# Low parts of the first two weight tiles of five stages: subtracted on GpSimd instead of added by a transfer

## The chip, the cores and the metric

One core of a Trainium2 chip runs the whole program. A core has a matrix engine (TensorE, PE in the rows; PEld is its loading of weights), three engines for elementwise work (VectorE or DVE, ScalarE or ACT, GpSimd or POOL), an engine that here only issues transfers (SyncE, SP), and DMA queues that move data. Each engine works its instructions off in order and waits on semaphores for what it needs from others. The metric is the time on the device in microseconds; the number compared is the median of several runs.

## The reference

Two layers of a transformer-like trunk. Each layer is a feed-forward block, a mixer and another feed-forward block, all of them added onto x:

```python
def ffn_sublayer(x, mod, k, g, w_in, w_out):
    h = modulated_norm(x, mod, k, g)
    gt, up = jnp.split(h @ w_in, 2, axis=-1)
    return x + 0.5 * mod[:, None, 3 * k + 2] * ((jax.nn.silu(gt) * up) @ w_out)

def trunk_layer(...):
    x = ffn_sublayer(x, mod, 0, norm_g[0], w_ffn_in[0], w_ffn_out[0])
    h = modulated_norm(x, mod, 1, norm_g[1])
    q, k, v, u_pool, u_conv, bg, cg = jnp.split(h @ w_in, IN_SPLITS, axis=-1)
    ...
    y = jnp.concatenate([attn, pool, conv], axis=-1) @ w_out
    x = x + mod[:, None, 5] * y
    x = ffn_sublayer(x, mod, 2, norm_g[2], w_ffn_in[1], w_ffn_out[1])
```

D_MODEL is 1024, D_FF 2816. The 128 context rows and the 512 latent rows share the weights, so the kernel treats them as 640 columns. Everything is float32.

## The kernel before

**Products in three parts.** A float32 weight tile is split into a high part wh, which TensorE's fast float32 form holds exactly, and a low part wl, the rest. An activation h is split the same way. `mm3` issues three matmuls for each product: wh times h's high part (L352), wh times h's low part (L353), wl times h's high part (L354). The 640 columns are worked in two halves of 320 (hf 0 and 1); x, transposed, lies in eight tiles of 128 x 640, x0 to x7.

**Where a weight's parts come from.** `load_cols` loads a tile of 128 x 1024 values into a buffer raw (an issue on SP, L181), and `split_w` splits it. ACT writes wh as a rounding copy of raw (L170). Without an engine given, ACT then writes wl = -wh (L173) and POOL issues a transfer that adds raw onto wl in memory (L174, the software queue q0). With an engine given, that engine computes wl = raw - wh in one instruction (L176). There are four buffers each for wh and wl and five for raw; a raw buffer is free for the next load when the adding transfer (or the subtraction) has read it.

**The stages.** ffn(0,0) to 530 us, mixer 0 to 755, ffn(0,2) to 1224, ffn(1,0) to 1681, mixer 1 to 1907, ffn(1,2) to the end. Each of the last five begins while the one before it ends: `update_x` adds the last products onto x tile by tile (DVE, L518, reading PSUM), `add_square` squares the tile on ACT (L251) and sums the squares on DVE (L252), TensorE sums over partitions (L375), and `rsqrt_newton` (ACT L361, DVE L362 to L364) makes the factor of the norm. A stage's first four weight tiles are loaded and split in the same microseconds.

**The head of a mixer.** Its h is made by DVE (L401, tmp from x), ACT (L416, high part) and DVE (L417, low part). The first `project` works two tiles of columns from 1024 on and two from 1536 on, four weight tiles in all.

**The head of an ffn.** h is made for two x tiles at a time (`seven`): DVE L480 and ACT L483 write full, ACT L473 copies the high part of the pair and DVE L474 subtracts the low part. The first pairs of the first half are made before the stage before has quite ended. `ups_by_half(0, 2)` takes the four weight tiles (j, s) with j and s 0 and 1, through `weights(j, s)`. The first ffn has another head (`first_tiles`).

**What sets the order.** The program is written in stages, but a scheduler with prices of its own sets the order of instructions on each engine's queue. Buffers come from pools, and an instruction waits on semaphores for its operands and buffers.

Of the kernel before, what the change touches and what calls it, by code (L numbers as in the profile page):

```python
# [17 lines left out]
P = 128  # L18
# [7 lines left out]
DFF = 2816  # L26
# [70 lines left out]
def trunk_kernel(ctx: ExitStack, tc: tile.TileContext, i: dict, o: dict):  # L97
    nc = tc.nc
# [18 lines left out]
    def slot(dt=F32, name="slot", shape=(2, T)):  # L117
        return slots.tile([P, *shape], dt, tag="slot", name=name)
# [17 lines left out]
    for b in range(T // P):  # L136
        s = slot(name="xin", shape=(D,))
# [26 lines left out]
    def split_w(raw, nk, width, eng=None):  # L164

        view = lambda t: t[:, : nk * width].rearrange("p (k c) -> p k c", k=nk)
        size, tag = (1024, "") if nk * width > 512 else (512, "s")
        h = view(whp.tile([P, size], F32R, tag="wh" + tag, name="wh", bufs=4 if tag == "" else 2))
        lo = view(wlp.tile([P, size], F32R, tag="wl" + tag, name="wl", bufs=4 if tag == "" else 2))
        nc.scalar.activation(h, raw, AF.Copy)  # L170
        if eng is None:

            nc.scalar.activation(lo, f32(h), AF.Copy, scale=-1.0)  # L173
            nc.gpsimd.dma_start(lo, raw, accum_op=ALU.add)  # L174
        else:
            eng.tensor_tensor(lo, raw, f32(h), op=ALU.subtract)  # L176
        return h, lo

    def load_raw(src, c0, width=P, raw=None):
        return raw_w(  # L180
            lambda raw: nc.sync.dma_start(raw, src[:, c0 : c0 + width].rearrange("(k p) c -> p k c", p=P)),  # L181
            src.shape[0] // P,
            width,
            raw,
        )
# [4 lines left out]
    def load_cols(src, c0, width=P, eng=None):  # L190
        return split_w(*load_raw(src, c0, width), eng)
# [364 lines left out]
    def ffn(l, f, n, hs, side, finish, nxt, first=None):  # L556
        w_in = i["w_ffn_in"][l, f]
# [1 line left out]
        gs = {}  # L559

        def weights(j, s):
            return load_cols(w_in, s * DFF + j * P)

        def part(ps, w, hf):

# [25 lines left out]
        def ups_by_half(j0, j1):  # L591

            ws = {(j, s): weights(j, s) for j in range(j0, j1) for s in range(2)}
            for hf in range(2):
                for j in range(j0, j1):
                    ps = [acc(), acc()]
                    for s in range(2):
                        for _ in part(ps[s], ws[j, s], hf):
                            pass
                    gated(j, hf, *ps)  # L600

        def up(j):
            ps = {}
            for s in range(2):
                w = weights(j, s)
                runs = []
                for hf in range(2):
                    ps[s, hf] = acc()
                    runs.append(part(ps[s, hf], w, hf))
                for _ in zip(*runs):  # L610
                    pass
            bias = None
            if first:
                bias, _ = shift_products(ps[0, 1], ps[1, 1])
            for hf in range(2):
                gated(j, hf, ps[0, hf], ps[1, hf], bias)
# [140 lines left out]
    def mixer(l, hs, finish, nxt):  # L757
# [19 lines left out]
        w_in = i["w_in"][l]  # L777
# [17 lines left out]
        def project(*tiles):  # L795

            runs = [(t, (hf,)) for hf in range(2) for t in tiles] if len(tiles) > 1 else [(tiles[0], (0, 1))]
            for ((wh, wl), evac), halves in runs:
                ps = {hf: acc() for hf in halves}
                for k in range(KD):  # L800
                    for hf in halves:
                        mm3(ps[hf][:, :HALF], wh[:, k, :], wl[:, k, :], *hs.part(k, hf), k == 0, k == KD - 1)
                    tick()
                for hf in halves:
                    evac(hf, ps[hf])

        def copy_to(dst):
            def evac(hf, ps):
                a, b = HALVES[hf]
                nc.scalar.activation(dst[:, a:b], ps[:, :HALF], AF.Copy)  # L810

            return evac


        u = slot(name="u")
# [5 lines left out]
        def product_to(m):  # L821
            def evac_z(hf, ps):
                a = HALVES[hf][0]
                for s, e, j in SEGS[hf]:
                    d = s + 2 - j
                    nc.vector.tensor_tensor(
                        zs[m][:, d : d + e - s], ps[:, s - a : e - a], u[:, m, s:e], op=ALU.mult
                    )

            return evac_z  # L830

        project(
            *[(load_cols(w_in, 1024 + m * P), copy_to(u[:, m, :])) for m in range(2)],
            *[(load_cols(w_in, 1536 + m * P), product_to(m)) for m in range(2)],
        )
        for m in range(2):
# [499 lines left out]
    for x, (l, n) in enumerate(steps):  # L1336
        last = x == len(steps) - 1
        fast = not last and steps[x + 1][1] != 1
        new = Seven() if fast else Plain()
        if last:  # L1340
            nxt = output
        else:
            heads = []

            def nxt(hf, t):
                if t < KD - 1:
                    return
                heads.append(norm_head(hf))
                if hf == 1 and fast:
                    seven(*steps[x + 1], new, heads)  # L1350
                elif hf == 1:
                    for h in range(2):
                        norm_tail(*steps[x + 1], h, new, heads[h])

        finish = nothing if last else squares
        if n == 1:
            mixer(l, hs, finish, nxt)
        else:
            ffn(l, n // 2, n, hs, spread(budget.get((l, n), 0), 1 if x else 4, x == 0), finish, nxt, None if x else first_tiles)
        hs = new  # L1360
# [30 lines left out]
```

## Time and profile before

| what | before |
|---|---|
| median of 3 runs | 2360.88 us (2357.27 to 2363.95) |
| the profiled execution | 2359.89 us |
| its span | 2358.1 us |
| granted TensorE clock, mean of the span | 0.993 |
| TensorE busy | 2302.1 us (98%) |
| VectorE busy | 1526.2 us (65%) |
| ScalarE busy | 1055.0 us (45%) |
| GpSimd busy | 123.9 us (5%) |
| adding transfers wl<-raw | 102 of 512 KB |

The profiled execution lies 1.0 us below the median. The page's "idle before" of a group of instructions says how long its engine stood just before them and for whom; of an engine that is busy 98% of the span, each such microsecond is one of the program's.

### The profile page before, as it was taken

Reading aid. Unit: us, or ns where it says so; the run is one execution under the profiler, and the core shown is the slowest. Engines: PE = TensorE matmul, PEld = TensorE weight load, DVE = VectorE, ACT = ScalarE, POOL = GpSimd, SP = SyncE. Lnnn points to the kernel's source line nnn. Section 1 sums busy time; section 2 is a strip of 40 time slices with the busy share of each in tenths; the row PEclk is TensorE's granted clock in tenths of the full one; section 3 lists DMA queues with packets and bytes.
Section 4 is the critical chain, followed back from the end, with each engine's and each line's share of the span. In section 5 each row is a group of like instructions: output and inputs, shape, how many; then the busy total and the mean of one; then the engine's idle time right before and its main releaser. Section 6 shows DMA issues by size and latency. Waiting matters only on the chain.

```text
span 2358.1 us, 40880 instructions
## 1 busy us (share of the span) xinstructions
PE 2302.1 (98%) x16594; PEld 2220.2 (94%) x16594; DVE 1526.2 (65%) x3133; ACT 1055.0 (45%) x1852; POOL 123.9 (5%) x157
## 2 busy tenths in 40 slices
PE   7899999999999999999999999999999999999999
PEld 6899999998978999999999999999898789999999
DVE  5546665556767756666667576675658676666674
ACT  4423233335767534343455343343556674344351
POOL 2101010001200000000000000000111000000000
PEclk9999999999999999999999999999999999999999
DMA  8858596727533544453544333433475242322321
GB/s 274 213 141 230 160 263 165 198 64 159 133 86 81 144 142 127 117 164 100 158 98 126 117 115 109 134 106 112 90 163 115 54 91 79 106 73 85 89 81 45
DMA packets 355988, 301.04 MB, mean 128 GB/s; under 512 B 27384, under 2 KB 303192, under 8 KB 355800
## 3 DMA queue, kind: packets, MB, share of 16 engines
q1 hardware_dynamic: 340932, 244.88, 34.5%
q0 software_dynamic: 14688, 53.48, 12.5%
q8 instruction: 130, 2.13, 0.4%
q14 instruction: 58, 0.48, 0.1%
q10 hardware_dynamic: 180, 0.07, 0.0%
HBM read 242.04 MB, written 2.88 MB: 104 GB/s over the span
## 4 chain that ended last, share of the span: by engine, by line
PE 82%; issue 7%; DMA 5%; DVE 4%; ACT 2%; POOL 0%; SPq 0%; ACTq 0%; POOLq 0%; DVEq 0%
PE acc L352 21%; PE acc L353 21%; PE acc L354 21%; PE mis L353 3%; PE mis L352 3%; PE mis L354 3%; DMA wl<-raw 2%; PE mis L275 2%; PE po L352 1%; DMA raw<-in_w_ffn_in 1%; PE po L353 1%; PE po L354 1%; DMA raw<-in_w_ada 1%; PE acc L1060 1%; PE mis L1111 1%
## 5 line engine op out<-in xcount | busy, mean ns | idle before, releaser
L352 PE MATMUL acc<-h,wh 128*128 128x320 f32 (+1 forms) x2808 | 878.2, 315 | 17.4 <-ACT h L416 5.4
L354 PE MATMUL acc<-h,wl 128*128 128x320 f32 (+1 forms) x2808 | 870.7, 311 | 10.5 <-DMA wl<-raw 10.5
L353 PE MATMUL acc<-h,wh 128*128 128x320 f32 (+1 forms) x2808 | 872.9, 312 | 4.5 <-DVE h L412 3.9
L170 ACT ACTIVATE wh<-raw 128x1024 fp32r<-128x1024 f32 (+2 forms) x332 | 306.2, 924 | 653.0 <-PE mis L353 289.8
L352 PEld LDWEIGHTS acc<-h,wh 128*128 128x128 f32 x2808 | 530.7, 190 | 33.1 <-issue 8.1
L354 PEld LDWEIGHTS acc<-h,wl 128*128 128x128 f32 x2808 | 531.3, 189 | 13.7 <-DMA wl<-raw 13.5
L353 PEld LDWEIGHTS acc<-h,wh 128*128 128x128 f32 x2808 | 531.7, 189 | 6.7 <-DVE h L412 4.1
L176 DVE TENSOR_TENSOR wl<-raw,wh 128x1024 fp32r<-128x1024 f32 (+2 forms) x228 | 222.2, 975 | 58.9 <-ACT wh L170 54.5
L352 PE MATMUL acc<-g,wh 128*128 128x320 f32 x832 | 258.2, 310 | 0.0
L353 PE MATMUL acc<-g,wh 128*128 128x320 f32 x832 | 258.0, 310 | 0.0
L354 PE MATMUL acc<-g,wl 128*128 128x320 f32 x832 | 257.3, 309 | 0.0
L170 ACT ACTIVATE wh<-sums 128x1024 fp32r<-128x1024 f32 x114 | 120.2, 1059 | 199.9 <-PE acc L353 90.7
L176 DVE TENSOR_TENSOR wl<-sums,wh 128x1024 fp32r<-128x1024 f32 x114 | 139.4, 1224 | 71.7 <-ACT wh L170 53.4
L174 POOL DMA_DIRECT2D wl<-raw x102 | 89.5, 877 | 1734.2 <-DVE x L518 967.8
L518 DVE SCALAR_TENSOR_TENSOR x<-acc,gate,x 128x128 f32<-128x128 f32 (+1 forms) x352 | 125.2, 394 | 84.5 <-PE acc L354 82.8
L353 PE MATMUL mis<-g,wh 128*128 128x320 f32 x576 | 177.9, 309 | 0.0
L354 PE MATMUL mis<-g,wl 128*128 128x320 f32 x576 | 177.8, 309 | 0.0
L352 PE MATMUL mis<-g,wh 128*128 128x320 f32 x576 | 177.8, 309 | 0.0
L352 PEld LDWEIGHTS acc<-g,wh 128*128 128x128 f32 x832 | 156.3, 188 | 1.8 <-issue 1.6
L354 PEld LDWEIGHTS acc<-g,wl 128*128 128x128 f32 x832 | 156.4, 188 | 0.2
L353 PEld LDWEIGHTS acc<-g,wh 128*128 128x128 f32 x832 | 156.3, 188 | 0.3
L311 DVE SCALAR_TENSOR_TENSOR sums<-raw,c,sums 128x512 f32<-128x512 f32 x196 | 135.2, 745 | 26.1 <-DMA raw<-in_w_ada 25.8
(208 smaller groups left out, 3177.1 us busy)
## 6 DMA issues: line engine op xcount, KB each, us to landing
raw<-in_w_ffn_in SPq DMA_DIRECT2D x176, 512.0 KB, 3.9
raw<-in_w_ada SPq DMA_DIRECT2D x128, 512.0 KB, 4.9
wl<-raw POOLq DMA_DIRECT2D x102, 512.0 KB, 5.5
raw<-in_w_ffn_out SPq DMA_DIRECT2D x48, 512.0 KB, 5.0
raw<-in_w_ffn_out SPq DMA_DIRECT2D x64, 320.0 KB, 3.8
raw<-in_w_in SPq DMA_DIRECT2D x20, 512.0 KB, 5.5
adaw<-in_w_ada SPq DMA_DIRECT2D x16, 512.0 KB, 9.7
raw<-in_w_in SPq DMA_DIRECT2D x16, 256.0 KB, 6.5
```

Source lines behind the costliest of these rows:

```text
L170: nc.scalar.activation(h, raw, AF.Copy)
L174: nc.gpsimd.dma_start(lo, raw, accum_op=ALU.add)
L176: eng.tensor_tensor(lo, raw, f32(h), op=ALU.subtract)
L275: last = nc.tensor.matmul(ps[32 * g : 32 * g + 32, 0:P], c2[:, 2 * q + k, :], r[:, k, g * P : (g + 1) * P], start=(q + k == 0), stop=(q + ...
L311: nc.vector.scalar_tensor_tensor(part[:, j, :], r[:, k, :], c, part[:, j, :], op0=ALU.mult, op1=ALU.add)
L352: nc.tensor.matmul(out, wh, xh, start=start, stop=False, skip_group_check=onto)
L353: nc.tensor.matmul(out, wh, xl, start=False, stop=False, skip_group_check=onto)
L354: return nc.tensor.matmul(out, wl, xh, start=False, stop=stop, skip_group_check=onto)
L518: nc.vector.scalar_tensor_tensor(xT[t][:, s:e], ps[:, s - a : e - a], gates[l][n][:, t, j : j + 1], xT[t][:, s:e], op0=ALU.mult, op1=ALU.add,)
L1060: nc.tensor.matmul(ps[:, :w], qs[2 * c + m][:, g, self.qc], self.kk[x][:, g, :], start=(x == 0), stop=(x == 1),)
L1111: nc.tensor.transpose(pt[:, (g * 2 + m) * P : (g * 2 + m + 1) * P], self.pr[m][:, g, x * P : (x + 1) * P], ident,)
```

## The change

Two calls get `eng=nc.gpsimd`. In an ffn these are the two weight tiles of j = 0 (gate and up) that `ups_by_half(0, 2)` takes; the first ffn doesn't come through this call for them. In a mixer they are the two tiles from column 1024 on. Five stages with two tiles each make ten weight tiles: for each, ACT's L173 and POOL's L174 go, and POOL gets an L176 of 128x1024.

```diff
         def weights(j, s):
-            return load_cols(w_in, s * DFF + j * P)
+            return load_cols(w_in, s * DFF + j * P, eng=nc.gpsimd if j == 0 else None)
...
         project(
-            *[(load_cols(w_in, 1024 + m * P), copy_to(u[:, m, :])) for m in range(2)],
+            *[(load_cols(w_in, 1024 + m * P, eng=nc.gpsimd), copy_to(u[:, m, :])) for m in range(2)],
             *[(load_cols(w_in, 1536 + m * P), product_to(m)) for m in range(2)],
```

On POOL the new instructions stand where the transfers were issued. On ACT, at the start of mixer 0 (sq is the square of an x tile), the rows before are

```order
L170 ACTIVATE wh_5545<-raw_5543 128x1024
L251 ACTIVATE sq_5312<-x1_93 128x320
L173 ACTIVATE wl_5546<-wh_5545 128x1024
L251 ACTIVATE sq_5329<-x2_94 128x320
L170 ACTIVATE wh_5552<-raw_5550 128x1024
L251 ACTIVATE sq_5346<-x3_95 128x320
L173 ACTIVATE wl_5553<-wh_5552 128x1024
L251 ACTIVATE sq_5363<-x4_96 128x320
L170 ACTIVATE wh_5559<-raw_5557 128x1024
```

and the rows after are

```order
L170 ACTIVATE wh_5545<-raw_5543 128x1024
L251 ACTIVATE sq_5312<-x1_93 128x320
L251 ACTIVATE sq_5329<-x2_94 128x320
L170 ACTIVATE wh_5551<-raw_5549 128x1024
L251 ACTIVATE sq_5346<-x3_95 128x320
L251 ACTIVATE sq_5363<-x4_96 128x320
L170 ACTIVATE wh_5557<-raw_5555 128x1024
```

The two negated copies are gone and nothing else has moved; the orders of DVE and TensorE are the same here, and mixer 1 is like it.

At the starts of the ffns the scheduler also orders ACT, DVE and TensorE anew. TensorE at the start of ffn(0,2) before, from the seventh product on (h_7944 and h_7956 are the first and second pair of h; wh_8068 and wl_8069 the second weight tile, wh_8075 and wl_8076 the third, wh_8082 the fourth):

```order
L352 MATMUL acc_8088<-h_7944,wh_8068 128x320
L353 MATMUL acc_8088<-h_7944,wh_8068 128x320
L354 MATMUL acc_8088<-h_7944,wl_8069 128x320
L352 MATMUL acc_8088<-h_7944,wh_8068 128x320
L353 MATMUL acc_8088<-h_7944,wh_8068 128x320
L354 MATMUL acc_8088<-h_7944,wl_8069 128x320
L352 MATMUL acc_8143<-h_7944,wh_8075 128x320
L353 MATMUL acc_8143<-h_7944,wh_8075 128x320
L352 MATMUL acc_8144<-h_7944,wh_8082 128x320
L353 MATMUL acc_8144<-h_7944,wh_8082 128x320
L352 MATMUL acc_8087<-h_7956,wh_8061 128x320
```

and after, from the seventh product on (here h_7942 is the first pair of h and h_7954 the second):

```order
L352 MATMUL acc_8083<-h_7954,wh_8059 128x320
L352 MATMUL acc_8084<-h_7942,wh_8065 128x320
L353 MATMUL acc_8084<-h_7942,wh_8065 128x320
L354 MATMUL acc_8084<-h_7942,wl_8066 128x320
L352 MATMUL acc_8084<-h_7942,wh_8065 128x320
L353 MATMUL acc_8084<-h_7942,wh_8065 128x320
L354 MATMUL acc_8084<-h_7942,wl_8066 128x320
L352 MATMUL acc_8084<-h_7954,wh_8065 128x320
L352 MATMUL acc_8139<-h_7942,wh_8071 128x320
L353 MATMUL acc_8083<-h_7954,wh_8059 128x320
```

Before, TensorE had sixteen products on the first pair ahead of the first one on the second pair; now it has six.

ACT in the same place, before (from the third weight tile's high part on):

```order
L170 ACTIVATE wh_8075<-raw_8073 128x1024
L251 ACTIVATE sq_7839<-x5_97 128x320
L173 ACTIVATE wl_8076<-wh_8075 128x1024
```

and after:

```order
L170 ACTIVATE wh_8071<-raw_8069 128x1024
L251 ACTIVATE sq_7888<-x5_97 128x320
L483 ACTIVATE full_7945<-full_7945,mods0_180 128x192
L483 ACTIVATE full_7945<-full_7945,mods0_180 128x128
L483 ACTIVATE full_7945<-full_7945,mods0_180 128x192
L173 ACTIVATE wl_8072<-wh_8071 128x1024
L251 ACTIVATE sq_7905<-x6_98 128x320
L473 ACTIVATE h_7954<-full_7945 128x2x320
```

The negated copy of the third weight tile now stands behind three L483, of which it had none ahead of it.

## Rows read from the trace of the kernel before

**Rows 1.** the page: engines (part 1); costliest groups (5): busy, mean ns, idle before

```profile
PE 2302.1 (98%) x16594; PEld 2220.2 (94%) x16594; DVE 1526.2 (65%) x3133; ACT 1055.0 (45%) x1852; POOL 123.9 (5%) x157
...
L354 PE MATMUL acc<-h,wl 128*128 128x320 f32 (+1 forms) x2808 | 870.7, 311 | 10.5 <-DMA wl<-raw 10.5
```

**Rows 2.** TensorE's waits, one row for each stage start in order: us, times, longest

```profile
PE acc L354 <- DMA wl<-raw: 1.5, 1, 1.5
PE acc L354 <- DMA wl<-raw: 1.7, 2, 1.2
PE acc L354 <- DMA wl<-raw: 3.2, 3, 1.7
PE acc L354 <- DMA wl<-raw: 0.3, 1, 0.3
PE acc L354 <- DMA wl<-raw: 2.1, 2, 1.6
```

**Rows 3.** instructions by line: ACT L173, and transfers of L174 to landing, min/median/max

```profile
L173 ACT ACTIVATE wl<-wh x102: 1039/1058/1071, 62.8 to 1942.4; 128x1024 fp32r<-128x1024 f32 x102
...
DMA to landing us min/median/max: 4.5/5.5/9.8
```

**Rows 4.** timeline near 20 us: start, us, engine, line; idle before in brackets

```profile
19.27 1.05 ACT L170 ACTIVATE wh<-raw 128x1024 fp32r<-128x1024 f32 x1
...
20.40 2.35 POOL L176 TENSOR_TENSOR wl<-raw,wh 128x1024 fp32r<-128x1024 f32 x1 [18.72 <-ACT wh L170]
...
20.45 2.51 DVE L401 SCALAR_TENSOR_TENSOR tmp<-x,gain,rr 128x192 f32<-128x192 f32 x1
...
22.71 2.45 POOL L176 TENSOR_TENSOR wl<-raw,wh 128x1024 fp32r<-128x1024 f32 x1
...
22.89 2.42 DVE L401 SCALAR_TENSOR_TENSOR tmp<-x,gain,rr 128x128 f32<-128x128 f32 x1
...
25.24 1.00 DVE L401 SCALAR_TENSOR_TENSOR tmp<-x,gain,rr 128x192 f32<-128x192 f32 x3
```

**Rows 5.** timelines at the start of mixer 0, and its chain of waits (last row)

```profile
519.70 1.05 ACT L170 ACTIVATE wh<-raw 128x1024 fp32r<-128x1024 f32 x1
...
520.94 0.49 DVE L364 SCALAR_TENSOR_TENSOR t<-t,r 128x320 f32<-128x320 f32 x1
...
531.26 0.49 DVE L252 TENSOR_TENSOR ssq<-ssq,sq 128x320 f32<-128x320 f32 x1 [0.75 <-ACT sq L251]
...
531.81 0.81 PE L375 MATMUL mis<-ssq,ones 128*128 128x320 f32 x2 [1.88 <-DVE ssq L252]
...
532.58 7.82 DMA wl<-raw
```

**Rows 6.** stretches of ffn(1,2): us, busy by engine, granted clock PEclk, transfers

```profile
1921.90:1927.30 5.40, 5.40 (x22) 5.40 (x22) 5.40 (x13) 5.40 (x15) 0.00 (x0) 0.50 0.00 0
1927.30:1940.00 12.70, 12.70 (x88) 12.70 (x88) 11.91 (x26) 10.13 (x16) 0.86 (x1) 0.99 0.16 32
```

**Rows 7.** timelines at the start of ffn(0,2)

```profile
754.82 0.86 POOL L174 DMA_DIRECT2D wl<-raw  x1 [2.68 <-ACT full L483]
...
756.14 0.30 PE L353 MATMUL acc<-h,wh 128*128 128x320 f32 x1
...
756.97 0.72 ACT L473 ACTIVATE h<-full 128x640 fp32r<-128x640 f32 x1
```

**Rows 8.** timelines at the start of ffn(1,0)

```profile
1220.64 0.81 DVE L474 TENSOR_TENSOR h<-full,h 128x640 fp32r<-128x640 f32 x1
...
1223.64 0.31 PE L353 MATMUL acc<-h,wh 128*128 128x320 f32 x1
```

**Rows 9.** the chain of waits at the start of ffn(1,2), and the timeline (last row)

```profile
1906.43 5.97 DMA wl<-raw
...
1912.47 6.58 DMA raw<-in_w_ffn_in
...
1921.50 0.90 PE L352 MATMUL acc<-h,wh 128*128 128x320 f32 x2 [3.51 <-ACT h L473]
```

## Prediction

> **What bounds the kernel now.** I read the page first, part 1 and then part 5, to see which engine has no slack: TensorE is busy in 98% of the span, and of its groups of products only the third one, the one that reads the low part wl, names an adding transfer as what it waited for, 10.5 us in ten waits [rows 1]. So anything gained or lost is gained or lost where TensorE stands still. I then read TensorE's waits stage by stage: the starts of the five later stages hold 1.5, 1.7, 3.2, 0.3 and 2.1 us of these waits, together 8.8 us; the rest of the 10.5 is in the first stage, which the change leaves alone [rows 2]. 8.8 us of 2359.89 is 0.37%, and it is the most that shorter low parts can give directly. Then I read the timelines of the starts, to see what VectorE (DVE) and ScalarE (ACT) do in the microseconds in which GpSimd (POOL) will now compute. They are the tail of one stage (x is updated tile by tile, squared and summed) and the head of the next (x is normalised into h): a chain that runs DVE, ACT, DVE and that TensorE waits for next.
>
> **What is removed.** Ten negated copies on ACT (L173) of about 1.06 us and ten adding transfers with 4.5 to 9.8 us from issue to landing, in the median 5.5 [rows 3]. None of the ten copies is itself what TensorE waits for; the transfers are, in part. In each start four adding transfers follow one another and only the first two go. The waits for the first two are the smaller ones; those for the third and fourth come because they are issued late: in mixer 0 the fourth is issued at 532.58 and takes 7.82 us [rows 5].
>
> **What is added.** Ten subtractions of 128x1024 on POOL. The trace has two of the same form, line and operands, of 2.35 and 2.45 us [rows 4], so each low part is there about 2.4 us after its high part instead of some 6.6 (1.06 + 5.5). That is the gain, up to 8.8 us.
>
> **What it does to VectorE.** While those two subtractions ran, DVE was in L401, an operation with two inputs in SBUF. The first L401 that met a subtraction took 2.51 us beside one of 2.35, the second 2.42 beside one of 2.45; the three right after, with no subtraction, took 1.00 together [rows 4]. So one DVE operation stood for the whole length of the subtraction, twice out of two. I take this as the price: a subtraction holds up a DVE operation with two inputs in SBUF from its start to its end, some 2.4 us, and all that is queued behind it on DVE, which works in order. The operations at the starts are of this kind: L252 (sum of squares), L364, L480, L474.
>
> The Trainium skill, SBUF — State Buffer, section "Who interferes with whom", states this as a rule: a VectorE instruction with two SBUF inputs and a GpSimd instruction that reads SBUF exclude each other for the whole instruction, and the second one waits. The four rows agree with it (2.51 us beside 2.35). By the rule the sum is the one below; were the four rows an accident, it would be that of the first rival.
>
> **Mixer starts.** The order of POOL, DVE and TensorE is the same there; ACT loses its two copies. ACT's first high part runs 519.70 to 520.75; the earlier subtraction began 0.08 us after its high part (19.27 + 1.05 = 20.32, then 20.40) [rows 4, 5]. So the first one runs about 520.83 to 523.2 and catches L364, due at 520.94. L364 ends at 523.4, the sum of squares behind it follows, the update of x's tile 2 behind that starts at 523.7 and its square on ACT at 524.3. In ACT's queue the second high part stands behind that square (524.7 to 525.75), so the second subtraction runs 525.8 to 528.2 and catches the sum of tile 3. From there each tile needs update, square and sum in turn, with high parts in between on ACT, about 1.5 us per tile: tile 7's sum starts at 534.0, not 531.26: +2.8 us. TensorE waits for exactly that sum already, 1.88 us [rows 5], so all of it is on the path. If the second subtraction falls into a gap of DVE, it is about +1.9; if starts slip the other way, 3.4. Against it stands the wait for the fourth adding transfer, 1.5 in mixer 0 and 0.3 in mixer 1 [rows 2]: it is issued later by the same 2.8, and it goes only if two transfers fewer in the queue make it quicker; I take half, 0.7 and 0.2. A longer stand also means more columns at the lower clock: after such a stand the granted clock was 0.50 for 5.40 us, in which 22 products ran, where 88 took 12.70 us at 0.99 [rows 6]; 22 at that rate are 3.2 us, so a full stretch costs 2.2. Mixers have short ones now; I add 0.5 each, from 0 to 1.0. Mixer 0: 2.8 - 0.7 + 0.5 = **+2.6** (0.4 to 4.0). Mixer 1: 2.8 - 0.2 + 0.5 = **+3.1** (1.5 to 4.0).
>
> **ffn(0,2).** Here the orders change. TensorE now runs only six products on h's first tile before one on its second, where sixteen stood before; ACT makes that second tile's high part (L473), which ran at 756.97 [rows 7]. Replaying the three queues row by row as for the mixer, I get two blocks of 2.4 us, at about 746.0 and 751.3, that push DVE's chain to it, and the copy ready at about 759.5. TensorE would get to that product at about 756.0 (it ran the eighth of the sixteen at 756.14 [rows 7]), so it loses up to 3.5 us there. The two waits of 1.7 go in exchange for it, but ACT's copy for the third tile is now behind three L483, so the third adding transfer, issued at 754.82 before [rows 7], goes out at about 758.9 and lands at about 764.2; its first product, 21 after the stand, is due at about 762.6. Net: that product's place in the work was reached at about 761.2 before, 763.4 to 764.2 after: **+2.6** (2.2 to 3.0, and 4.0 if the clock falls in the stand).
>
> **ffn(1,0).** The low part of h's first tile (L474, at 1220.64) has 2.2 us to spare before its product, which came at 1223.64 [rows 8]. The blocks move it to about 1224.7 to 1225.5, so TensorE stands 1.9; the 1.7 of the second adding transfer goes, and the fourth's product now stands later in TensorE's order, which takes up to 1.0. **+0.3** (-0.4 to +2).
>
> **ffn(1,2).** The longest stand, 3.5 us, hangs on a chain: third adding transfer issued at 1906.43, landed 5.97 later, only then is its raw buffer free for the next load, 6.58 us; ACT has to split that tile before it gets to h's L473, and TensorE waits until 1921.50 [rows 9]. As in ffn(0,2) the third transfer goes out some 4 us later; quicker landing gives back a part. The waits of 2.1 lie ahead of that and are swallowed. **+3.3** (1.0 to 4.5).
>
> **The sum.** 2.6 + 3.1 + 2.6 + 0.3 + 3.3 = 11.9 us. The profiled execution took 2359.89, 1.0 below the median of the runs shown (2360.88). 2359.89 + 11.9 = **2371.8**, 0.5% slower. The low ends add up to 4.7 (2364.6), the high ends to 18.5 (2378.4).
>
> **The rivals.** *The subtractions run beside DVE* (the change does what it is written for): DVE isn't held, the first two transfers' waits go, the last two meet an emptier queue. All of 8.8 gone is 2351; half, with the stand of ffn(1,2) as it is, is 2355.5; I put it at 2354, faster. It decides if a subtraction costs DVE less than the idle time that DVE has between x updates. For it: DVE isn't full at the mixer starts. Against it: both rows there are.
>
> *Held, but absorbed*: the subtractions start a few tenths earlier or later, fall into DVE's waits for the square or for the product, and each stand replaces a wait of about its size, as I have it for ffn(1,0). Then each stage is worth -1 to +1.5, in all 0 to +4: 2360 to 2364, say 2361.5. For it: in the ffn starts the waits removed (1.7, 3.2, 2.1) are near the stands added. Against it: in the mixers only 1.8 is there to be replaced, and 5.6 is added.
>
> *Held, and the clock falls each time*: every new stand is followed by a stretch at 0.50 as after 1921.90, 2.2 us each [rows 6]. Four such more than I counted give 8.8 less the 1.0 counted: 2379.6. For it: ffn(1,2) shows the pair of stand and slow stretch. Against it: the granted clock was 0.993 over the whole span, with the stands of all the starts in it.
>
> **How the numbers follow.** Forecast (2364.6 to 2378.4) 0.53; beside DVE 0.14; absorbed 0.22; clock 0.11. About 0.3% (7 us) is what a measurement of this kernel can tell from no change, so "faster" is below 2353.8 and "slower" above 2368.0. Faster: somewhat over half of the first rival, 0.09. Slower: the forecast without its lowest quarter, 0.42, the clock's 0.11 and a little of absorbed, 0.02: 0.55. Same: the other 0.36. The range goes from 2355, which leaves out most of the first rival (0.09), to 2378, which leaves out half of the last and the forecast's end (0.07).
>
> **What would show it.** In the profile after, DVE operations at the five starts that take 2.3 to 2.5 us instead of 0.35 to 0.55, one per subtraction; the wait for L252's sum in the mixers at 4 to 5 us instead of 1.88; TensorE waiting for L473 in ffn(0,2); in ffn(1,2) the late load landing after 1921. The waits for adding transfers should fall below 5 us. It would be wrong if DVE's longest operation stayed under 1 us (first rival), or if it is long and TensorE's waits at the starts still sum to what they were (second). If the stands are right and the time is off, the size of the slow-clock stretches is the term to look at.

## The result, and the profile after

The changed kernel took 2372.91 us in the median of 6 runs (2369.49 to 2379.61), the kernel before 2361.48 (2357.27 to 2363.95) beside it. The ratio is 1.0053, with a 95% interval of 1.0039 to 1.0066: slower, by about 12.5 us (the medians differ by 11.4). The forecast was 2371.8.

The profiled execution after has a span of 2368.4 us, 10.3 more than that of before. The two rows of the page that answer to [rows 1]:

```profile
PE 2306.3 (97%) x16594; PEld 2226.2 (94%) x16594; DVE 1544.7 (65%) x3133; ACT 1046.2 (44%) x1842; POOL 139.4 (6%) x157
...
L354 PE MATMUL acc<-h,wl 128*128 128x320 f32 (+1 forms) x2808 | 871.3, 311 | 2.2 <-DMA wl<-raw 2.1
```

The products on the low part now wait 2.1 us for adding transfers, not 10.5: what the change was to take away is gone, all but 0.4 of it at the five starts (the other 1.7 is in the first stage). TensorE stands for other things instead. TensorE's waits over the whole run (us in total, times, longest), the four rows that matter:

```profile
PE acc L352 <- ACT h L473: 10.1, 4, 3.3
PE mis L375 <- DVE ssq L252: 9.8, 2, 5.0
...
PE acc L352 <- ACT wh L170: 2.6, 2, 1.4
...
PE acc L353 <- DVE h L474: 1.4, 2, 1.2
```

The norm's matmul (L375) stood 1.88 us in each mixer [rows 5] and stands 5.0 and 4.8 now; the wait for h's high part (L473), one of 3.5 us before [rows 9], is 10.1 in four. Of the last two rows 1.4 us each are new, at the starts of ffn(1,0) and ffn(0,2).

Why, the timelines of GpSimd and VectorE at the starts show, the rows that answer to [rows 4]; two pairs of mixer 0, one of ffn(0,2) and one of ffn(1,0):

```profile
521.46 2.40 POOL L176 TENSOR_TENSOR wl<-raw,wh 128x1024 fp32r<-128x1024 f32 x1 [73.13 <-ACT wh L170]
...
521.57 2.63 DVE L364 SCALAR_TENSOR_TENSOR t<-t,r 128x320 f32<-128x320 f32 x1
...
526.66 2.39 POOL L176 TENSOR_TENSOR wl<-raw,wh 128x1024 fp32r<-128x1024 f32 x1 [2.80 <-ACT wh L170]
...
526.97 2.42 DVE L252 TENSOR_TENSOR ssq<-ssq,sq 128x320 f32<-128x320 f32 x1 [0.82 <-ACT sq L251]
...
748.58 2.39 POOL L176 TENSOR_TENSOR wl<-raw,wh 128x1024 fp32r<-128x1024 f32 x1 [34.98 <-ACT wh L170]
...
748.57 2.55 DVE L480 SCALAR_TENSOR_TENSOR full<-x,gain,t 128x128 f32<-128x128 f32 x1
...
1225.53 0.55 DVE L518 SCALAR_TENSOR_TENSOR x<-acc,gate,x 128x320 f32<-128x320 f32 x1
...
1225.70 2.40 POOL L176 TENSOR_TENSOR wl<-raw,wh 128x1024 fp32r<-128x1024 f32 x1 [3.44 <-ACT wh L170]
...
1226.01 2.43 DVE L252 TENSOR_TENSOR ssq<-ssq,sq 128x320 f32<-128x320 f32 x1
```

Each row of POOL has one of DVE beside it that ends 0.1 to 0.4 us after it: an L364, L252 or L480 of 2.42 to 2.63 us, where these take 0.34 to 0.49 alone. It is so for all ten subtractions of the change and for the two that were there before (there it is an L401). The row at 1225.53 is the exception that helps: L518 reads one operand from PSUM, began before that subtraction, ran 0.38 us into it and took its usual 0.55, and the subtraction took its usual 2.40.

Where the 10.3 us lie is read from the last product of each stage on TensorE. Before, and then after (start, us, engine, line):

```profile
529.62 0.31 PE L354 MATMUL acc<-g,wl 128*128 128x320 f32 x1
...
754.97 0.31 PE L354 MATMUL acc<-mix,wl 128*128 128x320 f32 x1
...
1223.36 0.31 PE L354 MATMUL acc<-g,wl 128*128 128x320 f32 x1
...
1681.24 0.31 PE L354 MATMUL acc<-g,wl 128*128 128x320 f32 x1
...
1906.62 0.31 PE L354 MATMUL acc<-mix,wl 128*128 128x320 f32 x1
```

```profile
530.25 0.31 PE L354 MATMUL acc<-g,wl 128*128 128x320 f32 x1
...
757.80 0.31 PE L354 MATMUL acc<-mix,wl 128*128 128x320 f32 x1
...
1228.68 0.31 PE L354 MATMUL acc<-g,wl 128*128 128x320 f32 x1
...
1685.99 0.31 PE L354 MATMUL acc<-g,wl 128*128 128x320 f32 x1
...
1915.10 0.31 PE L354 MATMUL acc<-mix,wl 128*128 128x320 f32 x1
```

The shifts are +0.6, +2.8, +5.3, +4.8 and +8.5, and +10.3 at the end, so the stages cost:

| stage | forecast | after, from these rows |
|---|---|---|
| up to mixer 0 (untouched) | 0 | +0.6 |
| mixer 0 | +2.6 | +2.2 |
| ffn(0,2) | +2.6 | +2.5 |
| ffn(1,0) | +0.3 | -0.6 |
| mixer 1 | +3.1 | +3.7 |
| ffn(1,2) | +3.3 | +1.8 |

### The profile page after: what moved, and what is told of

The parts are those of the page before. It is cut to its first block, busy times and chain, and to the rows that moved or that the text cites. A ratio compares the mean times of both kernels' runs of the same rounds, so it can differ in the third digit from the quotient of the medians.

```text
span 2368.4 us, 40876 instructions
## 1 busy us (share of the span) xinstructions
PE 2306.3 (97%) x16594; PEld 2226.2 (94%) x16594; DVE 1544.7 (65%) x3133; ACT 1046.2 (44%) x1842; POOL 139.4 (6%) x157
## 4 chain that ended last, share of the span: by engine, by line
PE 81%; DVE 7%; DMA 6%; ACT 3%; issue 3%; POOL 0%; SPq 0%; ACTq 0%; POOLq 0%; DVEq 0%
PE acc L352 20%; PE acc L353 20%; PE acc L354 20%; PE mis L354 3%; PE mis L353 3%; PE mis L352 3%; DMA raw<-in_w_ffn_in 2%; PE mis L275 2%; DMA wl<-raw 1%; PE po L1100 1%; PE po L352 1%; PE po L353 1%; DMA raw<-in_w_ada 1%; PE po L354 1%; PE mis L1111 1%
## 5 line engine op out<-in xcount | busy, mean ns | idle before, releaser
L352 PE MATMUL acc<-h,wh 128*128 128x320 f32 (+1 forms) x2808 | 879.5, 316 | 25.2 <-ACT h L473 10.1
L170 ACT ACTIVATE wh<-raw 128x1024 fp32r<-128x1024 f32 (+2 forms) x332 | 306.4, 924 | 644.3 <-PE mis L353 291.0
L176 DVE TENSOR_TENSOR wl<-raw,wh 128x1024 fp32r<-128x1024 f32 (+2 forms) x228 | 222.3, 975 | 56.2 <-ACT wh L170 51.8
L170 ACT ACTIVATE wh<-sums 128x1024 fp32r<-128x1024 f32 x114 | 120.3, 1059 | 204.0 <-PE acc L353 90.7
L176 DVE TENSOR_TENSOR wl<-sums,wh 128x1024 fp32r<-128x1024 f32 x114 | 139.4, 1224 | 73.0 <-ACT wh L170 54.0
L518 DVE SCALAR_TENSOR_TENSOR x<-acc,gate,x 128x128 f32<-128x128 f32 (+1 forms) x352 | 125.0, 393 | 82.2 <-PE acc L354 80.6
L518 DVE SCALAR_TENSOR_TENSOR x<-mis,gate,x 128x320 f32<-128x320 f32 x128 | 70.3, 549 | 108.1 <-PE mis L354 108.0
```

Source lines behind the costliest of these rows:

```text
L352: nc.tensor.matmul(out, wh, xh, start=start, stop=False, skip_group_check=onto)
L518: nc.vector.scalar_tensor_tensor(xT[t][:, s:e], ps[:, s - a : e - a], gates[l][n][:, t, j : j + 1], xT[t][:, s:e], op0=ALU.mult, op1=ALU.add,)
```

## The experiments

The theory: a subtraction on GpSimd holds a VectorE operation with two operands in SBUF, and with it the chain to the next stage. The main rivals: the new order at the ffn starts did it, or any work on GpSimd does it.

**The mixers alone, the ffns alone.** Each is one of the two edits of the change by itself:

```diff
-            *[(load_cols(w_in, 1024 + m * P), copy_to(u[:, m, :])) for m in range(2)],
+            *[(load_cols(w_in, 1024 + m * P, eng=nc.gpsimd), copy_to(u[:, m, :])) for m in range(2)],
```

> Only the two mixers' first two tiles are subtracted on GpSimd; the ffns keep their adding transfers. Theory (the subtraction holds VectorE for its whole length, and the stages are independent): the wait for the sum of squares (L375) is about 5 us in both mixers as in the changed kernel, the ffn starts keep their waits for adding transfers of 1.7, 3.2 and 2.1 us, and the total is 5 to 7 us above before. Rival (the loss comes from the scheduler's new order in the ffns, which the mixers don't have): within 1.5 us of before.

```diff
-            return load_cols(w_in, s * DFF + j * P)
+            return load_cols(w_in, s * DFF + j * P, eng=nc.gpsimd if j == 0 else None)
```

> Only the three later ffns' first two tiles are subtracted on GpSimd; the mixers are as before. Theory: stages independent, so the waits for L473 of the changed kernel come back (3.3 in ffn(0,2), 3.3 and 3.1 in ffn(1,2)), the mixers' L375 waits stay at 1.88, and the total is 3 to 5 us above before; this and the run with the mixers alone add up to the change's 10 within 2 us. Rival (all of the loss is in the mixers, and in the ffns each stand only replaces a wait): within 1.5 us of before.

The mixers alone: 1.0021 (1.0011 to 1.0030), +5 us, as the theory has it. The waits for L375 are 9.8 us in two, word for word those of the changed kernel, and the two mixers are 2.5 and 3.5 us longer than before by their last products, where the changed kernel has 2.2 and 3.7. The orders of VectorE and TensorE are those of before throughout: the new order of the ffns isn't needed for a loss. The ffns alone: 1.0041 (1.0024 to 1.0058), +9.7 us, where 3 to 5 were expected; the interval begins at 5.7. The waits are the expected ones, L473 9.9 us in four and L375 3.8 in two. The span of that profile (2370.8) contains 3.1 us that were lost in the first stage, which the edit doesn't touch, and a stand of 2.15 at 1154 us (for ScalarE, L671), far from a start; why the runs as a whole lost more than expected stays open. The two edits add up within the intervals (0.35% to 0.88% against 0.53%), not within the 2 us I had named.

**The hold alone.** The adding transfers stay, and GpSimd works beside them for nothing. In the first kernel it reads two operands, in the second it only fills (but for a one-column copy that ties it to the same moment). VectorE, ScalarE, TensorE and SyncE have the order of before in both, and both have the scratch tile and one buffer fewer. On GpSimd's own queue the scheduler put the reading, and part of the filling, ahead of the transfer's issue and not behind it, so the ten transfers go out 0.4 to 1.2 us after their L173 in the first kernel and 0.4 to 1.0 in the second, where it was 0.4 before.

```diff
-        if eng is None:
+        if eng is None or eng == "add":
...
-            nc.gpsimd.dma_start(lo, raw, accum_op=ALU.add)
+            nc.gpsimd.dma_start(lo, raw, accum_op=ALU.add); eng and nc.gpsimd.tensor_tensor(idle.rearrange("p (k c) -> p k c", k=nk), raw, f32(h), op=ALU.subtract)
...
```

> The kernel before with all its adding transfers; behind the issue of the transfer of each of the ten tiles GpSimd also computes raw - wh into a scratch tile that nobody reads (ten times 128x1024, some 2.4 us each). The other four engines have the same order as before; one buffer fewer in the large pool makes room. So nothing is gained and nothing else moves: it measures what the subtraction costs by being there. Theory (held): ten VectorE operations of 2.3 to 2.6 us, L375 waits of about 4 to 5 us in the mixers, total 6 to 18 us above before, since the waits for adding transfers stay. Rival (the loss comes from the new order, or from transfers issued later): VectorE's operations keep their 0.35 to 0.55 us and the total is within 1.5 us of before.

```diff
-            nc.gpsimd.dma_start(lo, raw, accum_op=ALU.add)
+            nc.gpsimd.dma_start(lo, raw, accum_op=ALU.add); eng and nc.gpsimd.tensor_copy(idle[:, :1], f32(h)[:, 0, :1]); [nc.gpsimd.memset(idle[:, :n], 0.0) for n in (1024, 1024, 384) if eng]
...
```

> As the run with the scratch subtraction, but GpSimd fills the scratch tile with zeros instead (a copy of one column that ties it to the same moment, then fills of 1024, 1024 and 384 columns, some 2 to 2.4 us in all): it works as long, at the same place, but reads no large operand. The order of the other four engines is that of before. Theory (it is GpSimd's reading of SBUF beside VectorE's second input that holds): VectorE's operations keep 0.35 to 0.55 us, total within 1.5 us of before. Rival (any GpSimd work of that length holds VectorE, or delays the next adding transfer in GpSimd's queue): 5 us or more above before, as with the subtraction. The Trainium skill, SBUF — State Buffer, section Who interferes with whom, says the former: a GpSimd instruction that only writes SBUF doesn't contend with a VectorE instruction with two SBUF inputs.

Reading: 1.0089 (1.0067 to 1.0112, four runs), 21 us slower. Filling: 1.0011 (0.9999 to 1.0023), no difference that can be told. Two pairs of rows of GpSimd and VectorE, first of the reading kernel, then of the filling one:

```profile
527.17 2.40 POOL L174 TENSOR_TENSOR idle<-raw,wh 128x1024 f32<-128x1024 f32 x1 [2.00 <-DVE ssq L252]
...
527.42 2.51 DVE L252 TENSOR_TENSOR ssq<-ssq,sq 128x320 f32<-128x320 f32 x1 [0.82 <-ACT sq L251]
```

```profile
746.93 0.96 POOL L174 MEMSET idle<- 128x1024 f32 x1
...
747.02 0.49 DVE L252 TENSOR_TENSOR ssq<-ssq,sq 128x320 f32<-128x320 f32 x1
```

The sum of squares takes 2.51 us beside the reading and 0.49 beside the fill; the reading kernel has ten VectorE operations of 2.4 to 2.7 us, the filling one has none that is longer than before. With the same order on the other four engines and transfers issued nearly as late, the difference of some 18 us between the two kernels is the price of ten holds. The change has ten holds too and lost 12.5, so by this estimate (18 or 21 less 12.5) the transfers that it saved gave back some 6 to 8 us; its ffn starts have another order, so the estimate is a rough one. Its gain was there, and it was smaller than its price. TensorE's waits for L375 were 9.9 us in two in the reading kernel, 3.8 in two in the filling one.

The Trainium skill, SBUF — State Buffer, section "Who interferes with whom", says that a VectorE instruction with two SBUF inputs contends with a GpSimd instruction that reads SBUF and not with one that only writes it, and that one with at most one SBUF input stays clear outside certain modes. These runs agree on all three: 2.51 us, 0.49 us, and 0.55 for L518 (x in SBUF, the product in PSUM) beside the subtraction at 1225.70.

**The hold in pieces.** Each of the ten subtractions is cut in four of 128x256; every engine but GpSimd has the order of the changed kernel.

```diff
-            eng.tensor_tensor(lo, raw, f32(h), op=ALU.subtract)
+            [(nc.gpsimd if eng == "pieces" else eng).tensor_tensor(lo[:, k : k + q], raw[:, k : k + q], f32(h)[:, k : k + q], op=ALU.subtract) for q in [2 if eng == "pieces" else nk] for k in range(0, nk, q)]
...
```

> The changed kernel, with each of the ten subtractions cut into four of 128x256 (some 0.6 us each). Every engine but GpSimd has the changed kernel's order word for word. Theory (the hold lasts for one GpSimd instruction, then VectorE gets in): no VectorE operation above about 1.2 us at the five starts; at the mixer starts, where VectorE has gaps, L375 waits of 3 to 4 us instead of 5.0; total 2 to 6 us below the changed kernel, still above before. Rival (the hold follows the amount that GpSimd reads, not the instruction): the same sum of holds at the same places, L375 waits of 5.0 and a total within 1.5 us of the changed kernel.

1.0011 (0.9995 to 1.0026) against before: some 10 us below the changed kernel by the two ratios, more than the 2 to 6 expected, and not to be told from before. The rows at the start of mixer 0:

```profile
523.00 0.74 POOL L176 TENSOR_TENSOR wl<-raw,wh 128x256 fp32r<-128x256 f32 x1 [74.84 <-ACT wh L170]
...
523.11 0.97 DVE L364 SCALAR_TENSOR_TENSOR t<-t,r 128x320 f32<-128x320 f32 x1
...
523.69 0.99 POOL L176 TENSOR_TENSOR wl<-raw,wh 128x256 fp32r<-128x256 f32 x1
...
524.00 1.02 DVE L252 TENSOR_TENSOR ssq<-ssq,sq 128x320 f32<-128x320 f32 x1
...
524.64 0.99 POOL L176 TENSOR_TENSOR wl<-raw,wh 128x256 fp32r<-128x256 f32 x1
...
524.95 0.54 DVE L518 SCALAR_TENSOR_TENSOR x<-acc,gate,x 128x320 f32<-128x320 f32 x1
```

No VectorE operation is held longer than a piece: the sum of squares at 524.00 takes 1.02 instead of 0.49, and the longest at the starts is an L474 of 1.36 that takes 0.81 alone (1.2 was the most expected). L518, with its PSUM operand, begins 0.31 us into a piece and takes 0.54. And the holding goes both ways: the first piece takes 0.74 us with nothing in its way, the next 0.99, behind the L364 that the first had held. The L375 waits are 4.5 in two (2.3 and 2.2), nearly those of before; so at a mixer start VectorE gets on between the pieces, and its gaps take most of what they cost. The waits for L473 remain, 8.1 in four. (The profiled run took 2368.0, 3 us above the median of this kernel.)

**The same ten on VectorE.**

```diff
-            return load_cols(w_in, s * DFF + j * P)
+            return load_cols(w_in, s * DFF + j * P, eng=nc.vector if j == 0 else None)
...
-            *[(load_cols(w_in, 1024 + m * P), copy_to(u[:, m, :])) for m in range(2)],
+            *[(load_cols(w_in, 1024 + m * P, eng=nc.vector), copy_to(u[:, m, :])) for m in range(2)],
```

> The same ten tiles, subtracted on VectorE itself: 0.98 to 1.22 us each by the rows of L176 on VectorE, in VectorE's own queue, and GpSimd has nothing to read there. The order of the ffn starts is a new one. Theory (what hurts is VectorE time on the chain, 2.4 us per tile on GpSimd, about 1.1 here): L375 waits of 3 to 4.5 us in the mixers, total 0 to 6 us above before, below the changed kernel. Rival (any subtraction on the chain costs the same, whatever its length): total as the changed kernel, 10 to 12 us above before.

0.9974 (0.9965 to 0.9984): 6 us faster than before, better than both sides had it. VectorE and TensorE at the start of mixer 0:

```profile
520.20 1.22 DVE L176 TENSOR_TENSOR wl<-raw,wh 128x1024 fp32r<-128x1024 f32 x1
...
531.14 0.81 PE L375 MATMUL mis<-ssq,ones 128*128 128x320 f32 x2 [1.89 <-DVE ssq L252]
```

The subtraction takes 1.22 us on VectorE, half of GpSimd's 2.4, and the wait behind it is 1.89, what it was before. I had expected L375 waits of 3 to 4.5 us; a VectorE operation of 1.22 us costs nothing there. In the list of TensorE's waits L473 doesn't appear any more, and the adding transfers that are left cost 8.2 us in six waits, not much less than the 10.5 of before. Of the 4.1 us between the two profiles (2354.0 against 2358.1) 3.0 lie in ffn(1,2): the stand of 3.51 for L473 [rows 9] became one of 2.92 for a transfer, and the granted clock behind it was 1.00, where it had been 0.50 for 5.40 us [rows 6]:

```profile
1916.47 0.42 PE L354 MATMUL acc<-h,wl 128*128 128x320 f32 x1 [2.92 <-DMA wl<-raw]
...
1916.20:1926.00 9.80, 8.82 (x58) 8.56 (x58) 9.53 (x22) 9.77 (x23) 0.00 (x0) 1.00 0.19 55
```

**A sixth raw buffer, on the kernel before.**

```diff
-    rawp = pool("raw", 5)
+    rawp = pool("raw", 6)
...
-    slots = pool("slots", 22)
+    slots = pool("slots", 21)
```

> The kernel before with six raw buffers instead of five and one buffer fewer in the large pool; nothing on GpSimd but the adding transfers of before. It tests the chain of ffn(1,2): there the late load waits for a raw buffer that the third adding transfer holds. Theory: with one more buffer that load is issued about 4 us earlier, the stand of 3.5 us for L473 and the slow stretch after it (about 2.5 us of loss) go, and the total is 3 to 6 us below before, with the waits for adding transfers where they were. Rival (the load waits for something else, or TensorE is held by the next thing right behind): L473 stand above 2 us, total within 1.5 us of before.

0.9981 (0.9970 to 0.9992), 4.5 us faster. The stand of 3.5 us for L473 is gone from the list and the adding transfers' waits stay at 9.5. The high part of the late tile, before and then in this kernel, is written some 6 us earlier, so the chain of [rows 9] did go through the buffer:

```profile
1919.07 0.63 ACT L170 ACTIVATE wh<-raw 128x512 fp32r<-128x512 f32 x1 [5.77 <-DMA raw<-in_w_ffn_in]
...
1912.92 0.63 ACT L170 ACTIVATE wh<-raw 128x512 fp32r<-128x512 f32 x1 [1.95 <-DMA raw<-in_w_ffn_in]
```

Right behind that place TensorE now stood 2.2 us for the first silu (L580), which took back part of what was gained. The scheduler also ordered VectorE, ScalarE and TensorE anew in places, so not all of the 4.5 us need be the buffer's.

**Adding transfers in halves, on the kernel before.**

```diff
-            nc.gpsimd.dma_start(lo, raw, accum_op=ALU.add)
+            [nc.gpsimd.dma_start(lo[:, k : k + q], raw[:, k : k + q], accum_op=ALU.add) for q in [nk // 2 if eng else nk] for k in range(0, nk, q)]
...
```

> The kernel before with every adding transfer of the first four tiles of the five stages issued as two halves of 128x512, which land one after the other; ACT's, VectorE's and SyncE's orders are those of before. It tries to get the change's gain without a subtraction: TensorE's first products on a tile need only the first half. Theory: the waits for adding transfers of 8.8 us at the five starts fall to 3 to 6, total 2 to 5 us below before. Rival (the halves share the queue's rate and the second issue costs as much as it saves): waits of 7 to 10 us, total within 2 us of before.

1.0005 (0.9996 to 1.0014), and 10.2 us of waits in eleven against 10.5 in ten, as the rival had it. Halving the transfer gains nothing.

**Both helpers, and VectorE for all four tiles.** The first kernel joins the edits of the two faster ones; the second gives all four tiles of each start to VectorE (j < 2, and the two from column 1536 on).

```diff
-    rawp = pool("raw", 5)
+    rawp = pool("raw", 6)
...
-            return load_cols(w_in, s * DFF + j * P)
+            return load_cols(w_in, s * DFF + j * P, eng=nc.vector if j == 0 else None)
...
```

> The ten subtractions on VectorE (as in the run with VectorE) and a sixth raw buffer (as in the run with six). Theory (the two help at different waits: the transfers of the first two tiles, and the late loads): total 7 to 12 us below before, the stand for L473 in ffn(1,2) below 1 us, L375 waits still 1.9. Rival (both act on the same stand, that of ffn(1,2), so the second adds nothing): 4 to 7 us below before.

```diff
-            return load_cols(w_in, s * DFF + j * P)
+            return load_cols(w_in, s * DFF + j * P, eng=nc.vector if j < 2 else None)
...
-            *[(load_cols(w_in, 1536 + m * P), product_to(m)) for m in range(2)],
+            *[(load_cols(w_in, 1536 + m * P, eng=nc.vector), product_to(m)) for m in range(2)],
...
```

> All four tiles at each of the five starts subtracted on VectorE, so that no adding transfer is left there. Theory (VectorE has gaps of some 3 us at a mixer start and about 2.5 of 15 us at an ffn start, so two subtractions of 1.22 us fit and four don't): the waits for adding transfers at the starts go, but L375 waits rise above 2.5 us or TensorE waits for h (L473, L474) by more than 3 us in sum, and the total is between 7 us below and 3 us above before. Rival (VectorE's time isn't what counts, only GpSimd's holding was): waits for h stay as with two tiles, and the total is 9 us or more below before.

Both helpers: 2348.53 us against 2362.55, 0.9937 (0.9923 to 0.9950). That is 14 us below before, more than the 12 expected at most and than the sum of the two (6 and 4.5, though within their intervals), and faster than both kernels of this case; the wait for L473 is 0.4 us, the L375 waits are 3.8 in two. All four tiles on VectorE: 0.9983 (0.9972 to 0.9994), 4 us below before and so no better than two (the intervals overlap). TensorE at the start of mixer 0 in that kernel:

```profile
532.15 1.02 PE L375 MATMUL mis<-ssq,ones 128*128 128x320 f32 x2 [2.90 <-DVE ssq L252]
```

No wait for an adding transfer is left at the starts, but the norm's matmul stands 2.90 instead of 1.88, and the silu of the first pair (L580) costs 6.8 us in three waits. Two subtractions fit into VectorE's gaps at a mixer start without a longer wait, four don't.

## Why the prediction was right

**The mechanism** was the forecast's: one VectorE operation held per subtraction, for the subtraction's length (2.4 to 2.6 us, forecast 2.3 to 2.5), read off the pair of rows at 20.4 and 22.7 [rows 4]. The run that only reads and the run that only fills turn the argument into a measurement.

**The mixers.** Forecast: tile 7's sum 2.8 us later, and all of it in the wait for L375. Measured: that wait went from 1.88 to 4.97 and 4.85, +3.1 and +3.0:

```profile
535.52 0.90 PE L375 MATMUL mis<-ssq,ones 128*128 128x320 f32 x1 [4.97 <-DVE ssq L252]
...
1691.14 1.44 PE L375 MATMUL mis<-ssq,ones 128*128 128x320 f32 x2 [4.85 <-DVE ssq L252]
```

The two holds came as replayed, on L364 and on the sum of tile 3, some 0.6 us later than written since the program reached this place 0.6 later. The transfer's wait (1.5 in mixer 0, 0.3 in mixer 1), of which I took half, went whole. The slower clock I had at 0.5 each, and it cost about twice that, in two places. These windows show them, first after, then before (us, busy and count by engine, granted clock in the column behind POOL's): L375 itself, then the first products of the mixers up to the end of the slow stretch.

```profile
535.50:536.95 1.45, 1.43 (x2) 0.50 (x2) 0.00 (x0) 0.39 (x1) 0.65 (x5) 0.50 1.05 198
539.64:543.80 4.16, 4.16 (x15) 4.16 (x16) 4.16 (x15) 2.56 (x7) 1.38 (x3) 0.50 0.97 217
1695.26:1700.95 5.69, 5.69 (x21) 5.69 (x22) 5.69 (x20) 3.22 (x9) 1.36 (x3) 0.50 0.99 216
```

```profile
531.80:532.62 0.82, 0.81 (x2) 0.30 (x2) 0.00 (x0) 0.38 (x1) 0.04 (x1) 1.00 1.21 263
535.29:538.30 3.01, 3.00 (x11) 3.01 (x12) 3.01 (x11) 1.54 (x4) 1.99 (x4) 0.50 1.15 279
1686.92:1692.00 5.08, 4.76 (x16) 4.36 (x17) 5.08 (x18) 3.07 (x8) 1.98 (x4) 0.50 1.11 278
```

The two matmuls of L375, on which h waits, take 1.43 us at a granted clock of 0.50, the lower of its two levels, where they took 0.81 at 1.00: 0.6 us in each mixer. The products run at 0.50 for 4.16 and 5.69 us of TensorE's time instead of 3.00 and 4.76; at half the rate the added 1.2 and 0.9 cost 0.6 and 0.5. Sum: 3.1 + 0.6 + 0.6 - 1.5 = +2.8 and 3.0 + 0.6 + 0.5 - 0.3 = +3.8, against 2.2 and 3.7 from the last products. So in mixer 0 the two misses, a transfer's wait that went whole and a clock that cost more, had opposite signs, and 0.6 of that sum isn't traced.

**ffn(0,2).** Forecast: TensorE loses up to 3.5 us at the seventh product, the third adding transfer goes out some 4 us later. The rows:

```profile
762.69 0.63 PE L352 MATMUL acc<-h,wh 128*128 128x320 f32 x1 [3.28 <-ACT h L473]
...
762.06 0.89 POOL L174 DMA_DIRECT2D wl<-raw  x1 [5.51 <-ACT sq L251]
```

The stand is 3.28, and 762.06 against 754.82 [rows 7] is 4.4 later when the 2.8 of the stage's own shift are taken off. The wait for that transfer, with which I came to 2.6, didn't follow: TensorE waited for no adding transfer in this stage. In its place the clock fell behind the stand, which I had only as an upper bound: 11 products in 2.5 us at 0.50, some 0.9 lost. New stands of 3.3 and 0.2, less the 1.7 that went, plus 0.9 make 2.7 at the start. The rest of the stage, which no edit touches, moved by single stands: at 829 us TensorE stood 1.37 for a row of the modulation (L265) and now 0.33, at 1151 it stood 0.2 for ScalarE (L671) and now 1.2. Such stands for L671 come and go in the other runs too (2.15 with the ffns alone, up to 0.8 with the mixers alone), and these two cancel. So 2.6 against 2.5 is right in size and right in its first step, the stand, and wrong in the second, which was the clock and not the transfer.

**ffn(1,0).** Forecast +0.3, measured -0.6. The new stands are 1.2 (L474), 1.4 (the high part of a weight tile, L170), 0.4 and 0.4, in sum 3.4, against 3.2 of removed waits: replaced nearly one for one, as forecast. I had seen only the first of them, and had the fourth's transfer for the balance. The other 0.8 lies at 1252 us, where before ten small products of the modulation (L275) and a wait stood between two products of the stage, and none do after.

**ffn(1,2)** is the term that was mis-sized: +1.8, not +3.3. The chain itself ran as forecast, seen in the chain of waits after (start, us, what) and the wait at its end:

```profile
1919.33 4.53 DMA wl<-raw
...
1923.92 6.51 DMA raw<-in_w_ffn_in
...
1933.19 0.64 PE L352 MATMUL acc<-h,wh 128*128 128x320 f32 x1 [3.08 <-ACT h L473]
```

Third transfer issued 4.4 us later than before (1919.33 against 1906.43, less the 8.5 of the stage's shift), landed in 4.53 instead of 5.97, next load 6.51; TensorE's stand ends at 1933.19, 3.2 later than the 1921.50 of [rows 9] after the same 8.5 are taken off. I left out three things. First, the stretch at the low clock behind that stand can change its length as well. Before it was 22 products in 5.40 us [rows 6]; after it is

```profile
1933.60:1936.40 2.80, 2.80 (x12) 2.80 (x12) 2.80 (x7) 2.80 (x8) 0.00 (x0) 0.50 0.00 0
```

12 products in 2.80 us. At the 0.144 us per product of the other row of [rows 6] the first is a loss of 2.2 us and the second one of 1.1, so 1.1 came back. Second, in its new order TensorE has more work done when it comes to that stand. From the last product of the mixer to the stand, before and after, and then a new stand for the first silu:

```profile
1906.75:1921.45 14.70, 9.18 (x58) 8.19 (x56) 8.11 (x19) 8.68 (x19) 1.41 (x2) 0.97 0.90 219
...
1915.22:1933.15 17.93, 11.50 (x65) 10.55 (x63) 11.46 (x28) 12.32 (x26) 1.72 (x2) 0.90 0.65 145
...
1940.64 0.42 PE L352 MATMUL acc<-h,wh 128*128 128x320 f32 x1 [0.57 <-ACT sg L580]
```

65 products instead of 58 are seven that needn't follow, 1.0 us. Third, the stand of 0.57 adds 0.6. Sum: 3.2 - 1.1 - 1.0 + 0.6 = 1.7, near the 1.8 measured. Ahead of all this lies a new stand of 3.28 us for the first L473 (1919.95) with a stretch of 2.3 us at the low clock behind it; they cost nothing of their own, since the stand that follows is set by the chain, as I had it for the 2.1 us of waits that stood there before.

**The rivals.** *Beside VectorE* is out by all ten rows. *Absorbed* is right for ffn(1,0) and for the run in pieces, and wrong for the rest. *The clock falls each time* is half right: it fell behind the new stands of ffn(0,2) and ffn(1,2) and already in the mixers' longer ones, but the stretches were short.

**The sum** was 11.9 against 10.3 between the two profiles and 12.5 by the ratio (by its interval 9 to 16). Of the profiles' 10.3, 0.6 lies ahead of the first edit. That the number agrees to about 1 us is partly luck: the terms were off by 0.1 to 1.5 with both signs. The mixers' upper bounds, added from their own parts (3.4 + 1.0), are 4.4 and not 4.0, so the range's high end was 0.8 too low by its own terms.

## What to carry to other kernels

Before work is moved to GpSimd because it is idle, list what VectorE does in the same microseconds: a GpSimd instruction that reads SBUF cost a VectorE operation with two SBUF operands the whole length of it, 2.4 us, however short that operation was; fills held none, and an operation with a PSUM operand wasn't held. Price the move by the chain that VectorE carries there, not by busy shares: GpSimd was busy 5% and VectorE 65%, and it cost 0.5%. If it has to be GpSimd, cut the instruction into pieces no longer than the gaps; if VectorE has gaps of that size anyway, VectorE itself does the work in half the time.

## What the runs showed of the hardware

The hold works in both directions: a piece of 128x256 on GpSimd took 0.74 us, and 0.99 when a VectorE operation with two SBUF operands stood ahead of it. GpSimd took 2.35 to 2.45 us for a subtraction that VectorE does in 1.22. An untouched stage isn't a fixed amount: the last product ahead of mixer 0 moved by 0.6 us after the change, and the first stage took about 3 us more in the profiles of the mixers alone and of the ffns alone, in neither of which it was edited; so a term of a microsecond or two is only to be read at its place, not from a span.
